# Second SSD layer, beginning: six stores for twenty, rows before totals, first masked copy behind the C tile

## The chip, the cores and the metric

The kernel runs on one core of a Trainium2 chip. Its time is device microseconds (us) of one execution. The core's engines work side by side, each through its own list of instructions in order: TensorE (PE in the profile, with PEld for its weight loads), VectorE (DVE), ScalarE (ACT), GpSimd (POOL), and SyncE (SP), which here issues DMA transfers and little else. An instruction starts when those ahead of it on its engine have started and the semaphores it waits for are there.

## The reference, cut to what matters

Two layers over 1024 latent and 256 context tokens, width 1024. The first is windowed attention, the second a bidirectional Mamba-2 (SSD) mixer. The change is in the second alone. Per direction d (0 forward, 1 backward) and chunk of 128 tokens it computes:

```python
dt = softplus(dt_raw + dt_bias)                    # 2 directions x 32 heads
a_cs = cumsum(dt * a, axis=chunk)                  # the decays
a_last = a_cs[:, :, -1]                            # the totals, one per chunk
states = einsum(bm, exp(a_last - a_cs), x * dt)
h_next = exp(a_last) * h + states                  # over chunks; context chunks come first
lmat = exp(where(lower, a_cs[q] - a_cs[s], -inf))  # 128 x 128 per head
y = (cm . bm) * lmat . (x * dt)  +  (cm . h) * exp(a_cs)
```

`x`, `bm` and `cm` come from one projection, a depthwise convolution over five tokens and a SiLU. There are 32 heads in 8 groups of 4, head width 64, state width 128, and 8 latent and 2 context chunks.

## The kernel before, in words

All matrix products of the projections are done three times, with a high and a low part of each operand (`wh`, `wl`, `uH`, `uL`). The second layer works group by group. `front(g)` is a generator that issues the projection of group g, one TensorE product at a time: the B tile (`bT`), two x tiles (`cacc`), the C tile (`cT`), then the gate z (L1129). For the B and x tiles a context part (`psD`, `cctx`) goes with the latent part (`pj2`, shown as `pj`). Behind each tile come the steps of `taps` (one ScalarE activation, four VectorE taps, L1007 and L1011), `silu` (a ScalarE tanh, L1018, and a VectorE product, L1019) and, for B and x, `natural` (TensorE transposes, L1058, and ScalarE copies out, L1061, to `xn` and `bn`). These steps wait in a queue `post`, from which `run(cost)` takes as the projection goes on.

The recurrence is in `states` (eleven jobs a group). A job is a weighting on GpSimd (`xw`, L1173), a TensorE product (`psD`, L1198), and for the first of a direction a ScalarE copy (`hx`, L1202), for the others a GpSimd decay by `eal` (L1178) and a VectorE addition (L1210). Then `slot(n)` computes the output of one chunk. It needs the matrix of decays `M`: per chunk two 256 KB loads from DRAM, `M` for the forward rows and `bw` for the backward rows, each row of `acs` broadcast over 128 partitions. GpSimd shifts `bw` (`offset`, L1226), VectorE copies `bw` into `M` under a mask (`merge`, L1230, COPY_PREDICATED), ScalarE takes four exponentials (`decays`, L1236). M and bw have two buffers each, and so have the weights `wr`, `wh`, `wl`.

Only once, while group 0 is projected, `dt_chain` makes the decays of all groups. Two VectorE scans (L986 for direction 0 on partitions 0 to 63, L987 for direction 1 on 64 to 127) write `w3` (named `sz` in the trace). Its 640 columns are five blocks of 128 tokens: two latent, one context, two latent, so that a partition row holds half a head's tokens. `decay` stores it to the DRAM tensor `acs` (64 rows of 1024); `total` takes each chunk's last value, its exponential `et` (named `tot`) is stored to the DRAM tensor `eald`, and one load (L953) brings this to all partitions as `eal`. `rows` asks for the rows of the first two chunks. Everything is float32. After the projection of group 0 the function `ssd` flushes `post`, finishes `states` and merges the first chunk's rows ahead of the loop over groups.

The order within an engine is not that of the code alone: a planner lays out each engine's list by dependences, code order and its own timeline, and `issue_after(x)` asks it to place an instruction behind x on x's engine, with no wait added.

Of the kernel before, what the change touches and what calls it, by code (L numbers as in the profile page):

```python
# [12 lines left out]
AF = mybir.ActivationFunctionType  # L13
ALU = mybir.AluOpType
# [3 lines left out]
P = 128  # L18
# [15 lines left out]
R = 4  # L34
HP = 64
# [24 lines left out]
OUT = 4 * 30 * 3 * N512  # L60
POST = 0.5
LATE = 3.0
DTPACE = 1.0
SEGS = (1.5, 2.0, 2.0, 2.2, 2.2)
_STOP = None
# [46 lines left out]
class Kernel:  # L112
# [13 lines left out]
    def t(self, pool, shape, dt, tag, bufs=None):  # L126
        self.n += 1
        kw = {"bufs": bufs or BUFS.get(tag, 1)}
        return pool.tile(shape, dt, tag=tag, name=f"{tag}_{self.n}", **kw)
# [795 lines left out]
    def dt_chain(self, keep, rows):  # L925

        nc, t, ps, p = self.nc, self.t, self.psA, self.ps_
        n = 640
        nb = n // P
        dt = self.dts  # L930
        w1, w2, w3, ea = [t(p, [P, KT // 2, 256], F32, y).rearrange("p a b -> p (a b)")[:, :n] for y in ("xn4", "sz", "sz", "xn4")]
        tot = t(self.pc, [P, 8], F32, "tot", 2)[:, :nb]
        et = t(self.pc, [P, 8], F32, "tot", 2)[:, :nb]
        blocks = lambda x: x.rearrange("p (c n) -> p c n", n=P)
        v, act = nc.vector, nc.scalar.activation

        def decay():
            for o in (0, 384):
                for y in range(4):
                    d, s = y // 2, (o // 384) * 512 + 256 * (y % 2)  # L940
                    nc.sync.dma_start(self.acs_d[32 * d : 32 * d + 32, s : s + 256], w3[32 * y : 32 * y + 32, o : o + 256])

        def total():
            v.tensor_copy(tot[:64], blocks(w3)[:64, :, P - 1])
            v.tensor_copy(tot[64:], blocks(w3)[64:, :, 0])
            act(et, tot, AF.Exp)
            for y in range(4):
                d, h = y // 2, y % 2
                row = self.eal_d[0][32 * d : 32 * d + 32]
                for o, c in ((0, 2 * h), (3, 4 + 2 * h)):  # L950
                    nc.sync.dma_start(row[:, c : c + 2], et[32 * y : 32 * y + 32, o : o + 2])
                nc.sync.dma_start(row[:, 8 + h : 9 + h], et[32 * y : 32 * y + 32, 2:3])
            nc.sync.dma_start(self.eal, self.eal_d.broadcast_to([P, 64, NCH + NCC]))  # L953

        def pairs(tile, d, c, step):
            return tile[:, c : c + step + 1 : step, 32 * d : 32 * d + 32]

        def turn(b):
            sl = slice(b * P, (b + 1) * P)
            c, step = {0: (0, 2), 1: (1, 2), 2: (8, 1), 3: (4, 2), 4: (5, 2)}[b]  # L960
            pt = t(ps, [P, 512], F32, "psX").rearrange("p (k d h r) -> p k d h r", k=4, d=2, h=2)
            srcs = (w1, ea, dt, w2) if c < NCH else (w1,)
            for k, src in enumerate(srcs):
                nc.tensor.transpose(pt[:, k].rearrange("p d h r -> p (d h r)"), src[:, sl], self.ident)
            for d in range(2):
                nc.scalar.copy(pairs(self.dtdec, d, c, step), pt[:, 0, d])
                if c < NCH:
                    nc.scalar.copy(pairs(self.eacs, d, c, step), pt[:, 1, d])
            if c < NCH:
                nc.scalar.copy(pairs(self.dtb, 0, c, step), pt[:, 2, 1])  # L970
                nc.scalar.copy(pairs(self.vf, 0, c, step), pt[:, 3, 0])
                nc.vector.tensor_sub(pairs(self.vd, 0, c, step), pt[:, 3, 1], pairs(self.vf, 0, c, step))

        steps = [
            lambda: v.scalar_tensor_tensor(w1, in0=dt, scalar=-1.0, in1=dt, op0=ALU.mult, op1=ALU.min),
            lambda: act(w1, w1, AF.Exp),
            lambda: v.tensor_scalar_add(w2, w1, 1.0),
            lambda: v.tensor_scalar_add(w3, w2, -1.0),
            lambda: (act(ea, w2, AF.Ln), v.tensor_sub(w1, w1, w3)),
            lambda: v.reciprocal(w3, w2),  # L980
            lambda: v.tensor_mul(w1, w1, w3),
            lambda: v.tensor_add(w1, w1, ea),
            lambda: v.scalar_tensor_tensor(dt, in0=dt, scalar=0.0, in1=w1, op0=ALU.max, op1=ALU.add),
            lambda: v.tensor_scalar_max(w2, dt, 1.0e-38),
            lambda: (act(w2, w2, AF.Ln), v.tensor_scalar(out=w1, in0=dt, scalar1=self.aneg, scalar2=None, op0=ALU.mult)),
            lambda: v.tensor_tensor_scan(out=w3[:64], data0=keep[:64], data1=w1[:64], initial=0.0, op0=ALU.mult, op1=ALU.add),  # L986
            lambda: v.tensor_tensor_scan(out=w3[64:, ::-1], data0=keep[64:, ::-1], data1=w1[64:, ::-1], initial=0.0, op0=ALU.mult, op1=ALU.add),  # L987
            decay,
            total,
            lambda: v.tensor_sub(blocks(w1), tot.unsqueeze(2).broadcast_to([P, nb, P]), blocks(w3)),  # L990
            lambda: act(w1, w1, AF.Exp),
            lambda: v.tensor_sub(w2, w2, w3),
            lambda: v.tensor_mul(w1, w1, dt),
            lambda: act(ea, w3, AF.Exp),
            rows,
        ]
        return steps + [lambda b=b: turn(b) for b in (2, 0, 4, 3, 1)]

    def dt_tail(self, raw, post, keep, rows):

        self.dt_raw(self.dts[:, 384:], raw, 256)
        post.extend([(DTPACE * x, [f]) for x, f in enumerate(self.dt_chain(keep, rows))])

# [11 lines left out]
    def silu(self, raw, acc):  # L1015

        nc = self.nc
        return [lambda: nc.scalar.activation(raw, acc, AF.Tanh),  # L1018
                lambda: nc.vector.scalar_tensor_tensor(acc, in0=raw, scalar=1.0, in1=acc, op0=ALU.add, op1=ALU.mult)]  # L1019

    def front(self, g, st, post, first=None, dt=None):

# [20 lines left out]
        def need(w):  # L1043
            while "l" not in w:
                post.pop()
# [7 lines left out]
        def natural(raw, acc, dst, o, n):  # L1053
# [6 lines left out]
            def ev(d, lo, hi):  # L1060
                nc.scalar.copy(d[:, :, o : o + P], raw[:, lo * P : hi * P].rearrange("p (c n) -> p c n", n=P))  # L1061

            for d, lo, hi in dst:
                steps.append(lambda lo=lo, hi=hi: tr(lo, hi))
                steps.append(lambda d=d, lo=lo, hi=hi: ev(d, lo, hi))
            return [(LATE, steps)]

# [8 lines left out]
        for n, (x, kind) in enumerate(tiles):  # L1076
# [37 lines left out]

            post.append((LATE, [done]) if nat else done)
        need(w)
# [28 lines left out]
    def ssd(self, c0):  # L1145
        nc, t, a = self.nc, self.t, self.a
# [9 lines left out]
        for x in range(2):  # L1156
            y = t(ps2, [P, 260], F32, f"y{x}")
# [4 lines left out]
        def hd(d, g):  # L1162
            return slice(32 * d + 4 * g, 32 * d + 4 * g + 4)
# [11 lines left out]
            return xw  # L1175

        def decay(hn, h, g, c, d):
            nc.gpsimd.tensor_tensor(hn, h, self.eal[:, hd(d, g), c].unsqueeze(2).broadcast_to([P, R, HP]), op=ALU.mult)  # L1178

        def flat(x):  # L1180
            return x.rearrange("p r h -> p (r h)")
# [1 line left out]
        def states(g, st):  # L1183
# [5 lines left out]
            for n, (d, c) in enumerate(jobs):  # L1189
                if n == 0:  # L1190
                    xw[0] = xweight(st, g, c, d)
                    yield
                if n + 1 < len(jobs):
                    xw[n + 1] = xweight(st, g, jobs[n + 1][1], jobs[n + 1][0])
                else:
                    st["xw"] = xweight(st, g, 0, 0)
                s = t(ps, [P, 512], F32, "psD")[:, :256]
                nc.tensor.matmul(s, B(st, c), flat(xw.pop(n)), start=True, stop=True)  # L1198
                sv = s.rearrange("p (r h) -> p r h", r=R)
                if n in (0, 2):  # L1200
                    h = t(ps2, [P, R, HP], F32, "hx")
                    nc.scalar.copy(h, sv)  # L1202
                else:
                    if n == 1:
                        hn = t(ps2, [P, R, HP], F32, "hf0")
                    else:
                        o = NCH - 1 if n == 3 else c - 1
                        hn = t(ps2, [P, R, HP], F32, f"hb{o if g % 2 == 0 else NCH - 1 - o}")
                    decay(hn, h, g, c, d)
                    nc.vector.tensor_add(hn, hn, sv)  # L1210
                    if n == 1:
                        st["hf"] = hn
                    else:
                        st["hb"][o] = h = hn
                yield
# [8 lines left out]
        def offset(n, bw):  # L1224
            g, c = divmod(n, NCH)
            nc.gpsimd.tensor_tensor(bw, bw, self.vd[:, c, 4 * g : 4 * g + 4].unsqueeze(2).broadcast_to([P, R, P]), op=ALU.add)  # L1226

        def merge(M, bw):

            nc.vector.copy_predicated(M, self.before.unsqueeze(1).broadcast_to([P, R, P]), bw)  # L1230
# [89 lines left out]
        fw, bw = {}, {}  # L1320
# [18 lines left out]
        for _ in chain:  # L1339
            pass  # L1340
        offset(0, bw[0])
        merge(fw[0], bw.pop(0))
        for half in range(2):
            decays(0, fw[0], half)
        self.tail = None
# [348 lines left out]
```

## Time and profile before

| | |
|---|---|
| median of three runs | 1809.46 us (1806.79 to 1813.08) |
| profiled execution | 1807.02 us, span 1805.3 us |
| TensorE busy | 1739.6 us (96%) |
| VectorE, ScalarE, GpSimd busy | 1181.8, 867.1, 799.0 us |
| mean granted TensorE clock | 0.993 |
| eight decay stores issued (SP) | from 794.12 us on |
| twelve stores of totals issued | 798.35 to 803.8 us |
| first row load issued | 803.93 us |
| load of `eal` issued, landed | 806.68 us, 8.0 us later |
| first masked copy | 815.05 us |

Times in the trace are us from the span's start. A timeline row has start, duration, engine, line, operation, out<-in, shapes and count; in brackets stands the idle time of the engine before it and what ended it. Buffer numbers are left out of names, so `pj` is any buffer of `pj2`. The chain of waits follows the last instruction back to what released it. Matmul ends are modelled, and rows of the same line and tile that follow each other are merged. A DMA's landing is counted from its issue.

### The profile page before, as it was taken

What the parts mean: (1) busy time and instruction counts of PE and PEld (TensorE: products, weight loads), DVE (VectorE), ACT (ScalarE), POOL (GpSimd) and SP (SyncE); (2) the same over time, 40 slices, a digit from 0 to 9 for tenths busy, and PEclk for the clock granted to TensorE, in tenths of its full rate; (3) what the DMA queues carried; (4) which work ended last, traced back from release to release, by engine and by line L of the source; (5) the groups of instructions that cost most, each with busy time, mean ns of one, the idle gap of its engine ahead of it and who ended that gap; (6) DMA issues with size and microseconds to landing.
All of it is one profiled execution on the core that took longest, in us unless ns stands there. A gap on an engine that the chain in (4) does not pass through costs nothing.

```text
span 1805.3 us, 28983 instructions
## 1 busy us (share of the span) xinstructions
PE 1739.6 (96%) x10319; PEld 1494.7 (83%) x10319; DVE 1181.8 (65%) x2115; ACT 867.1 (48%) x1906; POOL 799.0 (44%) x1068
## 2 busy tenths in 40 slices
PE   6899999999999999999999999999999999999997
PEld 2697788888888887778888898988889898888887
DVE  4634436778877885684776858577684867766734
ACT  3612237777777774452443525344353534544522
POOL 2331127555575545103454544645454464554411
PEclk9999999999999999999999999999999999999999
DMA  9558856444455436222222323222332322656533
GB/s 334 226 144 268 283 177 149 106 100 111 111 153 130 120 102 221 73 53 73 71 77 82 92 62 98 79 71 79 81 93 62 100 73 76 174 169 170 175 101 121
DMA packets 212495, 227.61 MB, mean 126 GB/s; under 512 B 16384, under 2 KB 149632, under 8 KB 212352
## 3 DMA queue, kind: packets, MB, share of 16 engines
q1 hardware_dynamic: 178288, 207.12, 38.0%
q0 software_dynamic: 34064, 18.65, 5.8%
q8 instruction: 81, 1.33, 0.3%
q14 instruction: 62, 0.51, 0.1%
HBM read 190.88 MB, written 35.13 MB: 125 GB/s over the span
## 4 chain that ended last, share of the span: by engine, by line
PE 81%; DVE 9%; ACT 4%; DMA 3%; issue 2%; SPq 1%; POOL 1%; DVEq 0%; ACTq 0%; POOLq 0%
PE pj L1095 17%; PE pj L1129 10%; PE pj L1527 7%; PE pj L246 6%; PE pj L247 6%; PE pj L248 6%; PE psD L1085 4%; PE psX L1281 3%; PE pt L684 3%; PE psD L1198 2%; PE pv L691 2%; PE pv L690 1%; PE S L659 1%; PE S L658 1%; PE psX L1249 1%
## 5 line engine op out<-in xcount | busy, mean ns | idle before, releaser
L246 PE MATMUL pj<-uH,wh 128*128 128x512 f32 (+1 forms) x712 | 257.4, 363 | 9.0 <-ACT uH L470 6.3
L247 PE MATMUL pj<-uL,wh 128*128 128x512 f32 (+1 forms) x712 | 243.3, 342 | 0.5 <-POOL uL L707 0.4
L248 PE MATMUL pj<-uH,wl 128*128 128x512 f32 (+1 forms) x712 | 242.4, 341 | 1.4 <-POOL wl L231 1.4
L1095 PE MATMUL pj<-uH,wl 128*128 128x512 f32 x512 | 172.7, 405 | 0.0
L1095 PE MATMUL pj<-uH,wh 128*128 128x512 f32 x512 | 171.4, 405 | 1.2 <-ACT bn L1061 0.7
L1095 PE MATMUL pj<-uL,wh 128*128 128x512 f32 x512 | 169.2, 402 | 0.0
L246 PEld LDWEIGHTS pj<-uH,wh 128*128 128x128 f32 x712 | 135.6, 191 | 36.2 <-ACT uH L470 7.7
L1129 PE MATMUL pj<-wh,uH 128*128 128x256 f32 x512 | 150.3, 294 | 9.1 <-ACT xn L1061 9.1
L1173 POOL TENSOR_TENSOR xw<-xn,dtdec 128x256 f32<-128x256 f32 x144 | 92.9, 650 | 141.6 <-PE psD L1198 107.1
L1129 PE MATMUL pj<-wh,uL 128*128 128x256 f32 x512 | 152.7, 298 | 0.0
L248 PEld LDWEIGHTS pj<-uH,wl 128*128 128x128 f32 x712 | 135.0, 190 | 18.6 <-POOL wl L231 2.3
L247 PEld LDWEIGHTS pj<-uL,wh 128*128 128x128 f32 x712 | 135.8, 191 | 16.0 <-issue 3.0
L1129 PE MATMUL pj<-wl,uH 128*128 128x256 f32 x512 | 146.7, 287 | 0.0
L689 DVE TENSOR_TENSOR pl<-pt,ph 128x512 fp32r<-128x512 f32 x168 | 114.1, 688 | 47.2 <-ACT ph L688 46.2
L231 POOL TENSOR_TENSOR wl<-wr,wh 128x512 fp32r<-128x512 f32 x76 | 100.2, 1322 | 86.1 <-ACT wh L229 85.2
L663 DVE CUSTOM_DVE_ANT_0 sm<-S,mask,nsink 128x640 f32<-128x640 f32 (+2 forms) x160 | 119.2, 773 | 19.8 <-PE S L659 12.6
L665 ACT ACTIVATE sm<-sm,nm 128x640 f32<-128x640 f32 (+2 forms) x160 | 118.6, 742 | 16.6 <-DVE nm L663 15.9
L688 ACT CAST ph<-pt 128x512 fp32r<-128x512 f32 x168 | 97.5, 586 | 56.0 <-PE pt L684 52.7
L229 ACT CAST wh<-wr 128x512 fp32r<-128x512 f32 (+1 forms) x116 | 74.7, 648 | 87.7 <-PE pj L247 63.5
L1095 PEld LDWEIGHTS pj<-uH,wl 128*128 128x128 f32 x512 | 95.3, 188 | 19.2
L1095 PEld LDWEIGHTS pj<-uL,wh 128*128 128x128 f32 x512 | 95.4, 188 | 18.7
L1129 PEld LDWEIGHTS pj<-wh,uH 128*128 128x128 f32 x512 | 98.7, 193 | 13.5 <-ACT xn L1061 12.1
(339 smaller groups left out, 4810.8 us busy)
## 6 DMA issues: line engine op xcount, KB each, us to landing
wr<-w_x SPq DMA_DIRECT2D x32, 512.0 KB, 4.6
M<-acs SPq DMA_DIRECT2D x64, 256.0 KB, 4.9
bw<-acs SPq DMA_DIRECT2D x64, 256.0 KB, 5.5
wr<-w_sk SPq DMA_DIRECT2D x24, 512.0 KB, 3.8
wr<-wg SPq DMA_DIRECT2D x40, 256.0 KB, 4.5
qs<-q POOLq DMA_DIRECT2D x40, 256.0 KB, 3.9
wada<-w_ada SPq DMA_DIRECT2D x16, 512.0 KB, 7.2
wr<-wq SPq DMA_DIRECT2D x32, 256.0 KB, 3.0
```

Of the source, the lines that this page charges most:

```text
L231: (eng or nc.vector).tensor_tensor(l, raw, h, op=ALU.subtract)
L246: self.nc.tensor.matmul(ps, lh, rh, start=first and i == 0, stop=False)
L247: self.nc.tensor.matmul(ps, lh, rl, start=False, stop=False)
L248: self.last_mm = self.nc.tensor.matmul(ps, ll, rh, start=False, stop=last and i == n - 1)
L663: nc.vector.tensor_tensor_reduce(out=sm[:, :W], in0=Sv, in1=self.mask[:, m0 : m0 + W], scale=-SCALE, scalar=self.nsink[:, 4 * j + r : 4 * ...
L665: nc.scalar.activation(sm[:, :W], sm[:, :W], AF.Exp, bias=nm[:, r : r + 1], scale=-1.0, accum_out=sums[:, r : r + 1])
L688: nc.scalar.copy(ph, ptf)
L689: nc.vector.tensor_sub(pl, ptf, ph)
L1095: nc.tensor.matmul(raw[:, 512 * i : 512 * i + 512], l[:, k, :], r[i][:, k, :], start=k + y == 0, stop=k == KT - 1 and y == 2)
L1129: nc.tensor.matmul(pj[:, c], l, r[:, k, :], start=c % 2 + q + k + y == 0, stop=c % 2 == 1 and q == 1 and k == 3 and y == 2)
L1173: nc.gpsimd.tensor_tensor(xw, X(st, c).rearrange("p (r h) -> p r h", r=R), self.dtdec[:, c, hd(d, g)].unsqueeze(2).broadcast_to([P, R, HP] ...
L1527: nc.tensor.matmul(banks[x], l[:, z, sl], r, start=k == 2 * qs[0] and y == 0, stop=k == 2 * qs[-1] + 1 and y == 2)
```

## The change

`decay` and `total` store two blocks, or five totals, of all 64 rows of a direction in one transfer: four stores of 2x32x256 for eight of 32x256, and two of 2x32x5 for twelve of 32x2 and 32x1. The totals lie in `eald` in the order of the blocks, and `EPOS` gives the column of each chunk. `rows` moves from the end of the chain to a place between `decay` and `total`. `silu` keeps its last product in `self.silu_last`, and the first chunk's `merge` is put behind it with `issue_after`; the last such product of the flush is the C tile's.

```diff
+EPOS = (0, 1, 5, 6, 3, 4, 8, 9, 2, 7)
...
         def decay():
-            for o in (0, 384):
-                for y in range(4):
-                    d, s = y // 2, (o // 384) * 512 + 256 * (y % 2)
-                    nc.sync.dma_start(self.acs_d[32 * d : 32 * d + 32, s : s + 256], w3[32 * y : 32 * y + 32, o : o + 256])
+            for d in range(2):
+                for o in range(2):
+                    dst = self.acs_d[32 * d : 32 * d + 32, 512 * o : 512 * o + 512].rearrange("r (h n) -> h r n", h=2)
+                    nc.sync.dma_start(dst, w3[64 * d : 64 * d + 64, 384 * o : 384 * o + 256])
...
             act(et, tot, AF.Exp)
-            for y in range(4):
-                d, h = y // 2, y % 2
-                row = self.eal_d[0][32 * d : 32 * d + 32]
-                for o, c in ((0, 2 * h), (3, 4 + 2 * h)):
-                    nc.sync.dma_start(row[:, c : c + 2], et[32 * y : 32 * y + 32, o : o + 2])
-                nc.sync.dma_start(row[:, 8 + h : 9 + h], et[32 * y : 32 * y + 32, 2:3])
+            for d in range(2):
+                nc.sync.dma_start(self.eal_d[0, 32 * d : 32 * d + 32].rearrange("r (h k) -> h r k", h=2), et[64 * d : 64 * d + 64])
             nc.sync.dma_start(self.eal, self.eal_d.broadcast_to([P, 64, NCH + NCC]))
...
             decay,
+            rows,
             total,
...
             lambda: act(ea, w3, AF.Exp),
-            rows,
         ]
...
-        return [lambda: nc.scalar.activation(raw, acc, AF.Tanh),
-                lambda: nc.vector.scalar_tensor_tensor(acc, in0=raw, scalar=1.0, in1=acc, op0=ALU.add, op1=ALU.mult)]
+
+        def prod():
+            self.silu_last = nc.vector.scalar_tensor_tensor(acc, in0=raw, scalar=1.0, in1=acc, op0=ALU.add, op1=ALU.mult)
+
+        return [lambda: nc.scalar.activation(raw, acc, AF.Tanh), prod]
...
-            nc.gpsimd.tensor_tensor(hn, h, self.eal[:, hd(d, g), c].unsqueeze(2).broadcast_to([P, R, HP]), op=ALU.mult)
+            nc.gpsimd.tensor_tensor(hn, h, self.eal[:, hd(d, g), EPOS[c]].unsqueeze(2).broadcast_to([P, R, HP]), op=ALU.mult)
...
         offset(0, bw[0])
-        merge(fw[0], bw.pop(0))
+        with self.tc.issue_after(self.silu_last.ins):
+            merge(fw[0], bw.pop(0))
```

In the built programs the lists of TensorE and GpSimd are the same in both. SP's list from the last stores of totals on, before (names are the program's tiles with their numbers; `wr<-w_x` are weight loads):

```order
L951 DMA eald_8741<-tot_8874 32x2 x2
L952 DMA eald_8741<-tot_8874 32x1
L1221 DMA M_9099<-acs_8737 128x4x128
L1221 DMA bw_9101<-acs_8737 128x4x128
L953 DMA eal_8736<-eald_8741 128x640
L1221 DMA M_9103<-acs_8737 128x4x128
L1221 DMA bw_9105<-acs_8737 128x4x128
L1030 DMA wr_9536<-w_x 128x1024
L1221 DMA bw_9599<-acs_8737 128x4x128
L1030 DMA wr_9620<-w_x 128x1024
```

and SP's list from the stores of the decays on, now:

```order
L942 DMA acs_8737<-sz_8871 2x32x256 x4
L1221 DMA M_9003<-acs_8737 128x4x128
L1221 DMA bw_9005<-acs_8737 128x4x128
L1221 DMA M_9007<-acs_8737 128x4x128
L1221 DMA bw_9009<-acs_8737 128x4x128
L949 DMA eald_8741<-tot_8874 2x32x5 x2
L950 DMA eal_8736<-eald_8741 128x640
L1030 DMA wr_9522<-w_x 128x1024
L1030 DMA wr_9606<-w_x 128x1024
L1221 DMA bw_9585<-acs_8737 128x4x128
```

All four row loads now stand ahead of the stores of the totals, and the third chunk's `bw` stands behind one weight load more.

VectorE's list from the first masked copy on, before (`cacc_9091` is the second x tile, `cT_9227` the C tile):

```order
L1230 COPY_PREDICATED M_9099<-before_8738,bw_9101 128x512
L972 TENSOR_TENSOR vd_8732<-psX_9179,vf_8731 128x2x32
L972 TENSOR_TENSOR vd_8732<-psX_9198,vf_8731 128x2x32
L1019 SCALAR_TENSOR_TENSOR cacc_9091<-pj_2194_9090,cacc_9091 128x1024
L1038 TENSOR_TENSOR wl_9331<-wr_9318,wh_9329 128x1024
L1011 SCALAR_TENSOR_TENSOR cT_9227<-pj_2208_9226,cw_8721,cT_9227 128x1022
```

and VectorE's list from the x tile's product to the same copy, now:

```order
L1017 SCALAR_TENSOR_TENSOR cacc_9084<-pj_2198_9083,cacc_9084 128x1024
L1038 TENSOR_TENSOR wl_9317<-wr_9304,wh_9315 128x1024
L1008 SCALAR_TENSOR_TENSOR cT_9213<-pj_2208_9212,cw_8721,cT_9213 128x1022
L1008 SCALAR_TENSOR_TENSOR cT_9213<-pj_2208_9212,cw_8721,cT_9213 128x1023
L1210 TENSOR_TENSOR hf_2218_9283<-hf_2218_9283,psD_9281 128x256
L1008 SCALAR_TENSOR_TENSOR cT_9213<-pj_2208_9212,cw_8721,cT_9213 128x1023
L1008 SCALAR_TENSOR_TENSOR cT_9213<-pj_2208_9212,cw_8721,cT_9213 128x1022
L1017 SCALAR_TENSOR_TENSOR cT_9213<-pj_2208_9212,cT_9213 128x1024
L1230 COPY_PREDICATED M_9003<-before_8738,bw_9005 128x512
L1210 TENSOR_TENSOR hb_2228_9326<-hb_2228_9326,psD_9324 128x256
```

The copy has moved from ahead of the x tile's product to behind the C tile's. ScalarE's list, before, from the tanh of the x tile on:

```order
L1018 ACTIVATE pj_2194_9090<-cacc_9091 128x1024
L1236 ACTIVATE M_9099<-M_9099,vf_8731 128x128 x4
L1061 COPY xn_2160_8759<-psD_9056 128x2x128
L1034 CAST wh_9329<-wr_9318 128x1024
L1007 ACTIVATE cT_9227<-pj_2208_9226,cb_8724,cw_8721 128x1024
```

and ScalarE's list from the context copy on, now:

```order
L1061 COPY xn_2160_8759<-psD_9049 128x2x128
L1034 CAST wh_9315<-wr_9304 128x1024
L1004 ACTIVATE cT_9213<-pj_2208_9212,cb_8724,cw_8721 128x1024
L1061 COPY xn_2158_8757<-pj_2198_9083 128x4x128
L1202 COPY hx_9270<-psD_9268 128x256
L1061 COPY xn_2159_8758<-pj_2198_9083 128x4x128
L1019 ACTIVATE pj_2208_9212<-cT_9213 128x1024
L1202 COPY hx_9297<-psD_9295 128x256
L1236 ACTIVATE M_9003<-M_9003,vf_8731 128x128 x4
L1137 ACTIVATE sz_9463<-pj_2223_9306 128x1024
```

The four exponentials have moved from ahead of the context copy to behind the second state copy. Nothing else moves on either engine.

## The prediction

> **What bounds the kernel.** First the page: TensorE works 96% of the span, so only what lets it stand, or run at a lower clock, counts.
>
> ```profile
> PE 1739.6 (96%) x10319; PEld 1494.7 (83%) x10319; DVE 1181.8 (65%) x2115; ACT 867.1 (48%) x1906; POOL 799.0 (44%) x1068
> ```
>
> All that the change touches lies between 794 and 832 us, so next I read the chain that ended last there, in order of time (start, us, what).
>
> ```profile
> 807.07 9.10 DMA M<-acs
> 816.17 0.97 ACT M L1236 x3
> ...
> 817.30 1.04 ACT wh L1034
> 818.35 1.10 ACT cT L1007
> 819.45 0.48 ACT xn L1061
> ...
> 819.98 1.12 PE pj L1058 x4
> ...
> 821.95 5.08 PE pj L1129 x30
> ...
> 831.73 2.87 PE pj L1129 x24
> ```
>
> The chain leaves TensorE for a transfer, runs through ScalarE and comes back at 819.98. The timelines of TensorE, VectorE, ScalarE and GpSimd (start, us, operation, and in brackets the idle time ahead of it) tell why.
>
> ```profile
> 814.26 0.62 PE L1095 MATMUL pj<-uH,wl 128*128 128x512 f32 x2
> 817.19 0.66 PE L1058 MATMUL pj<-ident,cacc 128*128 128x128 f32 x4 [2.31 <-DVE cacc L1019]
> 818.14 1.22 PE L1198 MATMUL psD<-xw,bn 128*128 128x256 f32 x2 [0.29 <-POOL xw L1173]
> 820.88 1.06 PE L1198 MATMUL psD<-xw,bn 128*128 128x256 f32 x2
> 821.77 0.58 PE L1129 MATMUL pj<-wh,uH 128*128 128x256 f32 x1
> ```
>
> ```profile
> 808.52 1.27 DVE L1011 SCALAR_TENSOR_TENSOR cacc<-pj,cw,cacc 128x1022 f32<-128x1022 f32 x1
> 815.05 0.73 DVE L1230 COPY_PREDICATED M<-before,bw 128x512 f32<-128x512 int32 x1 [5.26 <-POOL bw L1226]
> ...
> 815.92 1.22 DVE L1019 SCALAR_TENSOR_TENSOR cacc<-pj,cacc 128x1024 f32<-128x1024 f32 x1
> ...
> 819.67 2.59 DVE L1011 SCALAR_TENSOR_TENSOR cT<-pj,cw,cT 128x1022 f32<-128x1022 f32 x2
> 822.17 0.41 DVE L1210 TENSOR_TENSOR hf<-hf,psD 128x256 f32<-128x256 f32 x1
> ...
> 831.83 0.42 DVE L1210 TENSOR_TENSOR hb<-hb,psD 128x256 f32<-128x256 f32 x1 [4.36 <-PE psD L1198]
> ```
>
> ```profile
> 810.73 1.10 ACT L1018 ACTIVATE pj<-cacc 128x1024 f32<-128x1024 f32 x1
> 815.87 1.28 ACT L1236 ACTIVATE M<-M,vf 128x128 f32<-128x128 f32 x4 [4.04 <-DVE M L1230]
> 817.05 0.35 ACT L1061 COPY xn<-psD 128x256 f32<-128x256 f32 x1
> ...
> 836.26 1.02 ACT L1137 ACTIVATE sz<-pj 128x1024 f32<-128x1024 f32 x1 [8.39 <-PE pj L1129]
> ```
>
> ```profile
> 813.97 1.04 POOL L1226 TENSOR_TENSOR bw<-bw,vd 128x512 f32<-128x512 f32 x1 [72.63 <-DMA bw<-acs]
> 817.48 1.19 POOL L1173 TENSOR_TENSOR xw<-xn,dtdec 128x256 f32<-128x256 f32 x2 [2.47 <-ACT xn L1061]
> ...
> 820.27 0.62 POOL L1178 TENSOR_TENSOR hf<-hx,eal 128x256 f32<-128x256 f32 x1
> ```
>
> The first masked copy (L1230) waits on VectorE for rows that are still in flight; the product of the x tile (L1019, cacc) stands behind it in order, and TensorE's transposes wait for that product 2.31 us. ScalarE waits 4.04 us for the copy too, with the context copy (817.05) and all that follows queued behind its four exponentials. There is a second price, in the windows of TensorE (length, then busy time of PE, PEld, DVE, ACT, POOL, granted clock, DMA share, GB/s):
>
> ```profile
> 781.00:785.00 4.00, 1.72 (x11) 0.86 (x9) 4.00 (x6) 3.18 (x4) 0.00 (x0) 1.00 0.00 0
> 814.76:818.17 3.41, 0.80 (x6) 0.45 (x5) 2.09 (x4) 2.30 (x6) 0.94 (x3) 1.00 0.58 104
> 818.17:821.58 3.41, 2.80 (x8) 1.72 (x8) 3.17 (x3) 2.48 (x5) 1.88 (x3) 0.50 0.73 208
> 821.58:824.99 3.41, 3.41 (x16) 3.23 (x16) 3.38 (x4) 0.13 (x1) 1.24 (x2) 0.50 0.48 177
> ```
>
> After the stretch with 0.80 us of work the granted clock is 0.50 for 6.8 us.
>
> **The change, part by part.** *Masked copy moved.* VectorE's product now needs only the tanh, which ends at 810.73 + 1.10 = 811.83, and VectorE, free from 809.8 but for two small subtractions. It runs from 811.9 to 813.1, before TensorE is free at 814.26 + 0.62 = 814.88. So the first transposes start at 814.9 and the 2.31 us are gone. Late next is ScalarE. Its weight cast (817.30) takes the buffer that the product of the C tile reads until about 814.5, and cannot start sooner; from it to the second transposes are 819.98 - 817.30 = 2.68 us, so those start at 817.2, **2.8 us** earlier. From them to the first L1129 are 821.77 - 819.98 = 1.79 us at half clock; at full clock four transposes take 0.66 (row 817.19), the copy that follows some 0.57, with handing over 1.3. L1129 starts at 818.5, 3.3 earlier: **0.5 us** more. The fifteen L1129 matmuls up to 825.0 (the last window has sixteen, one of them a state product's) took 3.22 us; at the full rate, 2.87 / 24 = 0.12, they take 1.80: **1.4 us** more.
>
> The clock term rests on there being no drop: from 814.9 TensorE has transposes (0.4 to 0.66) and a state product (0.43 at full clock), then about 1.3 us of waiting up to 817.2. It is then busy some 2.0 of 3.41 us (59%). The stretch from 781 to 785 was busy 1.72 of 4.00 (43%) and kept its clock at 1.00.
>
> *Where the copy goes.* It costs VectorE 0.73 us after the C tile's product, and the exponentials cost ScalarE 1.28. Behind it in VectorE's order stands the addition that idled 4.36 us (831.83), behind the exponentials the tanh that idled 8.39 us (836.26). Both covers are longer than the cost, also 4.7 us earlier since TensorE's products, which they wait for, move along. Were the cover gone, the price would be 0.73 and 1.28. The next row load (bw of the third chunk) waits for the copy and goes behind one weight load on SP's queue; it is used only in the second chunk, tens of us later: nothing.
>
> *Stores and rows on SP's queue.* Prices come from the DMA view, issues by tile (size, median us to landing), packets in two short windows (packets, MB, share of 16 engines), and SP's own rows:
>
> ```profile
> M<-acs SPq DMA_DIRECT2D x64, 256.0 KB, 4.9
> ...
> h<-h SPq DMA_DIRECT2D x16, 256.0 KB, 2.6
> ...
> wr<-w_x SPq DMA_DIRECT2D x32, 512.0 KB, 4.6
> ```
>
> ```profile
> q1 hardware_dynamic: 246, 0.12, 96.0%
> ```
>
> ```profile
> q1 hardware_dynamic: 96, 0.07, 13.5%
> ...
> acs<-sz SPq DMA_DIRECT2D x4, 32.0 KB, 1.5
> ```
>
> ```profile
> 794.12 4.14 SPq L941 DMA_DIRECT2D acs<-sz  x8
> ...
> 803.93 0.39 SPq L1221 DMA_DIRECT2D M<-acs  x1
> ```
>
> Twenty stores are twenty issues of about 0.42 us on SP (803.93 - 794.12 = 9.8 us with the gaps); six cost about 3. No engine waits for SP's issuing itself, so the saving counts only in when rows and totals land. Four decay stores go out from 794.1, the last two after the second scan (795.6), and land by 796.2 + 1.5 = 797.7. The rows are asked for then, 6 us sooner, and are no longer late for anything. The totals pay: their stores are queued behind four row loads of 512 packets. In the window from 807.5 to 809 such packets passed at 246 in 1.5 us, 3.1 us a load; so the fourth lands 4.9 + 3 x 3.1 = 14.2 us after the first is issued, the totals' stores 1.4 us later at most, and the load of eal takes 2.6 to 4.6 us (the rows of 256 and 512 KB; it has 320). From 797.7 that is 815.9 to 817.9. eal is first read by GpSimd's decay (820.27 before, about 817.5 now); its result, 0.62 on GpSimd and 0.42 on VectorE later, must be there when TensorE comes to the third state product, thirty L1129 after 818.5, at 822.1. So eal may land as late as 820.9 at no cost: I take nothing, and keep 0 to 2.8 us for the range (rival A). Reading eal by another column changes no size.
>
> Sum: 2.8 + 0.5 + 1.4 = **4.7 us** less. After 825 TensorE works on without a gap to 832 and everything behind hangs on it, so the shift is kept. The profiled execution took 1807.02 us (span 1805.30 and 1.7 around it), which gives 1802.3; it lies 2.4 us under the median of three, 1809.46, and against the median it is **1804.8 us**. A difference under 0.3% (5.4 us) can hardly be told here from no change: the three runs alone span 6.3 us.
>
> **Rivals.** *A, totals late, gain partly lost.* Each new store has the target form 2x32x256 against 64 source rows. If its 64 packets go out on two DMA engines and not sixteen, they queue: 96 packets took 13.5% of 16 x 2 us, 45 ns each, or 67 ns if the 32 tiny ones took none. Four stores then need 4 x 32 x 0.045 to 0.067 = 5.8 to 8.6 us from the first packet at about 794.95, the rows start at 800.7 to 803.5, and eal lands at 818.9 to 823.7. Beyond 820.9 each us is one us of TensorE: 0 to 2.8, middle 1.4, time 1806.2 us. For it speaks the shape; against it that no store here shows such a queue and the margin of 3 us. The Trainium skill (DMA: Bandwidth & Descriptors, section "Why a DMA increments its semaphore by 16 and not by 1") states that a transfer is split over the largest number of engines up to 16 that divides the slowest dimension of both sides, here 2 and 64, hence two engines. No run so far shows this, and by that rule rival A's landing holds instead of 817.
>
> *B, slower.* The same queue past the point where it takes all: eal landing after 820.9 + 4.7 = 825.6. One engine for all four stores would do it: 4 x 64 x 0.045 to 0.067 = 11.5 to 17.2 us, eal at 824.7 to 832.3, a stall of 3.8 to 11.4 us in which the clock falls again (another 1.4): net 0.5 to 8.1 us slower, middle 4, time 1813.5 us. Against it: the stores' target has two halves.
>
> *C, the clock falls all the same.* With 59% busy the granted clock may still drop at some 818.2 and stay for 6.8 us; 6.5 us of L1129 at half rate lose 3.25, leaving 4.7 - 3.2 = 1.5: 1808.0 us. For it: 43% is one case only. The Trainium skill (TensorE: Matmul & The Clock Gate, "Part 1: The HAM clock gate") has a free-running window of about 3.4 us; twice 3.41 us in the trace agrees. By that rule the phase differs between runs, and a run of the old kernel without the drop would leave a gain of 2.8.
>
> **How the numbers follow.** Forecast 0.57, A 0.25, C 0.10, B 0.08. The forecast's 1804.8 is 0.8 us short of the bound at 1804.0, and the profiled execution suggests that the median of before is a high one, so I give it a little over even odds of passing the bound (0.33), A a third (0.08), C little (0.01): faster 0.42. B gives slower, and noise a little more: 0.09. The rest, 0.49, is within 0.3%. Range: runs scatter by 3 us around a median, so 1800.3 below; above it takes in A, C and B's near end, 1810.0.
>
> **What would show it.** In the changed kernel's timeline: the x tile's product on VectorE near 812 with no wait for bw; the first transposes at once behind the C tile's matmuls; the second near 817; L1129 at 0.12 us from the start and a granted clock of 1.00 throughout; the copy idle-free behind the C tile's product. The landing of eal decides A and B: GpSimd's first decay waits for a DMA if it is late, and TensorE's third state product waits behind it. I would be wrong if decay stores take longer than 3 us more to land, or if something after 850, hung on a transfer and not on TensorE, eats the shift.

## The result, and the profile after

The changed kernel took 1806.33 us in the median of 19 runs (1801.31 to 1811.95), the kernel before 1811.43 us in the median of 19 runs (1805.89 to 1814.45). The ratio of the runs is 0.9977, with a 95% interval of 0.9968 to 0.9986: 4.2 us less (2.5 to 5.8). This ratio, and not the quotient of the two medians, which lie 5.1 us apart, is used below. The forecast was 4.7 us less than a median of 1809.46. The interval holds 4.7 us, but also the 2.8 that the wait alone would give; how the gain is made up is read from traces, one of each kernel.

The profiled execution after took 1801.31 us, span 1799.6, which is 5.7 us under the span before. Of these, 1.8 us were there before the change begins: the second decay scan starts at 792.30 and not at 794.12, after a first layer that ran a little faster. The changed stretch gave 4.7, and the very end took 0.8 back (below). So the changed stretch is read against the second scan: a time that was forecast on the trace of before is met if the new trace shows it 1.82 us earlier.

TensorE's share in the page, then the chain that ended last (start, us, what), in the kernel after:

```profile
PE 1736.7 (97%) x10319; PEld 1493.0 (83%) x10319; DVE 1180.8 (66%) x2115; ACT 867.6 (48%) x1906; POOL 797.9 (44%) x1068
```

```profile
812.62 0.49 ACT wh L1034
...
813.57 1.20 ACT cT L1004
814.77 0.48 ACT xn L1061
...
815.30 0.67 PE pj L1058 x4
...
815.99 0.60 ACT xn L1061
...
816.63 3.86 PE pj L1129 x30
820.49 0.43 PE psD L1198 x2
...
842.92 0.22 PE psX L1247 x2
```

No transfer stands in it any more. It leaves TensorE at 812.6 for ScalarE's cast, the C tile's activation and one copy, and is back for good at 816.63. The first and the second transposes are two groups of four products (L1058) on the second x tile. The timelines of TensorE, VectorE, ScalarE and GpSimd after, at the places that the prediction named:

```profile
812.88 0.60 PE L1058 MATMUL pj<-ident,cacc 128*128 128x128 f32 x4
...
815.30 0.66 PE L1058 MATMUL pj<-ident,cacc 128*128 128x128 f32 x4 [1.38 <-ACT xn L1061]
...
816.63 0.39 PE L1129 MATMUL pj<-wh,uH 128*128 128x256 f32 x1 [0.24 <-ACT xn L1061]
```

```profile
810.02 1.23 DVE L1017 SCALAR_TENSOR_TENSOR cacc<-pj,cacc 128x1024 f32<-128x1024 f32 x1 [0.71 <-ACT pj L1019]
...
821.70 1.22 DVE L1017 SCALAR_TENSOR_TENSOR cT<-pj,cT 128x1024 f32<-128x1024 f32 x1 [1.43 <-ACT pj L1019]
822.84 0.74 DVE L1230 COPY_PREDICATED M<-before,bw 128x512 f32<-128x512 int32 x1
825.30 0.42 DVE L1210 TENSOR_TENSOR hb<-hb,psD 128x256 f32<-128x256 f32 x1 [1.72 <-PE psD L1198]
```

```profile
823.61 1.28 ACT L1236 ACTIVATE M<-M,vf 128x128 f32<-128x128 f32 x4 [1.64 <-DVE M L1230]
829.73 1.02 ACT L1137 ACTIVATE sz<-pj 128x1024 f32<-128x1024 f32 x1 [4.83 <-PE pj L1129]
```

```profile
804.93 1.04 POOL L1226 TENSOR_TENSOR bw<-bw,vd 128x512 f32<-128x512 f32 x1 [66.95 <-DVE vd L969]
...
815.60 0.62 POOL L1178 TENSOR_TENSOR hf<-hx,eal 128x256 f32<-128x256 f32 x1 [0.20 <-ACT hx L1202]
```

The x tile's product (cacc, 810.02) waits for its tanh alone, the first transposes (812.88) follow the C tile's products without a wait, and the idle time that is left on TensorE is 1.38 us ahead of the second transposes, for ScalarE's copy. The copy under the mask (822.84) stands behind the C tile's product, and both engines still idle behind it, 1.72 and 4.83 us. GpSimd's shift of bw (804.93) waited for VectorE's `vd` and no longer for a transfer, and its first decay (815.60) for ScalarE's `hx`, not for `eal`.

TensorE's windows after (columns as before):

```profile
812.00:815.41 3.41, 2.03 (x12) 1.41 (x11) 1.72 (x2) 2.79 (x4) 2.49 (x3) 1.00 0.13 54
815.41:818.82 3.41, 3.17 (x24) 2.77 (x25) 3.37 (x4) 0.69 (x2) 1.86 (x3) 1.00 0.54 154
```

The emptiest stretch is busy 2.03 of 3.41 us, and the granted clock stays at 1.00.

SP's issues after:

```profile
792.30 2.54 SPq L942 DMA_DIRECT2D acs<-sz  x4
795.90 0.38 SPq L1221 DMA_DIRECT2D M<-acs  x1
799.36 0.38 SPq L1221 DMA_DIRECT2D bw<-acs  x1
...
800.33 0.51 SPq L1221 DMA_DIRECT2D bw<-acs  x1
800.88 2.16 SPq L949 DMA_DIRECT2D eald<-tot  x2
807.07 0.34 SPq L950 DMA_DIRECT2D eal<-eald  x1
```

The DMA view after, packets from 793.4 to 796.9, and below it of before, from 794.5 to 796.5:

```profile
DMA packets 120, 0.12 MB, mean 34 GB/s; under 512 B 3, under 2 KB 120, under 8 KB 120
...
q1 hardware_dynamic: 120, 0.12, 12.7%
```

```profile
DMA packets 105, 0.07 MB, mean 37 GB/s; under 512 B 32, under 2 KB 105, under 8 KB 105
```

The window of after holds stores of decays only: 12.7% of 16 engines is 2.0 engines' worth, and among 120 packets 3 are small ones; before, 32 of 105 were. In the trace's single packets each new store is two streams of 46 ns a packet of 1 KB, one packet behind another, with two small completion writes where a store before had sixteen. The four stores' last packet passes at 800.2. The first row load is issued at 795.90, while the stores still run: the first store's completion writes passed at 795.39 and 795.48, and the load waits only for the store of its own quarter of `acs`. The one for `bw` waits until 799.36.

What the end took back is in the chain, TensorE's last two products, before and then after:

```profile
1796.82 0.71 PE psX L380 x2
```

```profile
1790.23 1.24 PE psX L381 x2
```

The same two products took 0.53 us more. Before, the granted clock fell to 0.50 only at 1797.79, behind them; after, it fell at 1789.12, ahead of them. Nothing of the change lies there; the stretch is nearly idle in both.

### The profile page after: what moved, and what is told of

Its sections match the earlier page's. It is cut to its first block, busy times and chain, and to the rows that moved or that the text cites. A ratio compares the mean times of both kernels' runs of the same rounds, so it can differ in the third digit from the quotient of the medians.

```text
span 1799.6 us, 28962 instructions
## 1 busy us (share of the span) xinstructions
PE 1736.7 (97%) x10319; PEld 1493.0 (83%) x10319; DVE 1180.8 (66%) x2115; ACT 867.6 (48%) x1906; POOL 797.9 (44%) x1068
## 3 DMA queue, kind: packets, MB, share of 16 engines
q8 instruction: 81, 1.33, 0.3%
## 4 chain that ended last, share of the span: by engine, by line
PE 81%; DVE 9%; ACT 4%; DMA 2%; issue 2%; POOL 0%; SPq 0%; DVEq 0%; ACTq 0%; POOLq 0%
PE pj L1095 18%; PE pj L1129 10%; PE pj L1528 7%; PE pj L247 6%; PE pj L248 6%; PE pj L249 6%; PE psD L1085 4%; PE pt L685 3%; PE psX L1281 3%; PE pv L692 2%; PE psD L1198 2%; PE pv L691 2%; PE S L660 1%; PE S L659 1%; PE psX L1249 1%
## 5 line engine op out<-in xcount | busy, mean ns | idle before, releaser
L1129 PE MATMUL pj<-wh,uH 128*128 128x256 f32 x512 | 149.6, 292 | 9.4 <-ACT xn L1061 9.4
L1129 PE MATMUL pj<-wh,uL 128*128 128x256 f32 x512 | 152.1, 297 | 0.0
L1129 PE MATMUL pj<-wl,uH 128*128 128x256 f32 x512 | 146.1, 285 | 0.0
L1129 PEld LDWEIGHTS pj<-wh,uH 128*128 128x128 f32 x512 | 98.0, 191 | 13.7 <-ACT xn L1061 12.2
```

The source lines that it names most:

```text
L1129: nc.tensor.matmul(pj[:, c], l, r[:, k, :], start=c % 2 + q + k + y == 0, stop=c % 2 == 1 and q == 1 and k == 3 and y == 2)
```

## The experiments

What a kernel did to the changed stretch is measured from the start of the second decay scan (VectorE) to the start of the first chunk's first product (TensorE, L1247): behind it TensorE's timeline shows no wait for the next 70 us in either trace. In TensorE's timeline this is 55.17 us before and 50.45 after, 4.72 less. (The expectations give 55.33 and 50.62, which are the chain's rows for the same product; the chain starts it 0.16 later.) Before, after and three of the others were timed in many runs, the rest in one, where only the stretch is read; in all, the stretch is that of one traced execution. In the table all columns but the last are us after the start of the second scan.

| kernel | first L1129 | third state product | first chunk's product | masked copy | first decay by `eal` | ratio to before |
|---|---|---|---|---|---|---|
| before | 27.65 | 32.75 | 55.17 | 20.93 | 26.15 | |
| after | 24.33 | 28.03 | 50.45 | 30.54 | 23.29 | 0.9977 [0.9968, 0.9986] |
| place of the copy alone | 24.36 | 28.05 | 50.48 | 30.77 | 23.85 | 0.9986 [0.9973, 0.9999] |
| after without that place | 24.35 | 28.05 | 50.48 | 13.80 | 23.31 | 0.9974 [0.9961, 0.9987] |
| six stores alone | 26.27 | 30.28 | 52.71 | 17.12 | 24.92 | one run |
| rows early alone | 24.35 | 28.05 | 50.48 | 14.24 | 24.68 | one run |
| after, totals three copies later | 24.33 | 28.03 | 50.45 | 31.12 | 24.96 | one run |
| after, totals six copies later | 24.35 | 32.39 | 56.41 | 37.42 | 31.26 | one run |
| before, the wait filled with products | 27.69 | 32.11 | 53.81 | 21.41 | 26.66 | one run |
| after, second copy ahead of the activation | 23.76 | 26.98 | 49.89 | 30.73 | 23.30 | 0.9964 [0.9949, 0.9980] |

### The copy's place alone

On the kernel before, only the masked copy is put behind the C tile's product; stores and rows stay.

```diff
-        merge(fw[0], bw.pop(0))
+        with self.tc.issue_after(self.silu_last.ins):
+            merge(fw[0], bw.pop(0))
```

> The kernel before with one edit alone: the first masked copy behind the C tile's product; twenty stores and late rows stay. Measure: from the start of the second scan on VectorE to the first product of the first chunk on TensorE (L1247), 55.33 us before and 50.62 in the changed kernel. Theory: the copy's place in VectorE's list is the cause and is enough; bw lands as late as before, GpSimd's shift of it ends near 815 and the weighting that follows is late by under 1 us, which is hidden: 50.6 to 51.2 us, and about 0.2% off the time. Rival: the late rows still bind through GpSimd, whose shift of bw stands ahead of the weighting: 52.5 us or more, at most half of the gain.

Measured: 50.48, all of the stretch's gain, and 0.9986 of the time before. GpSimd's shift still waits for its rows, and delays the weighting behind it:

```profile
813.75 1.04 POOL L1229 TENSOR_TENSOR bw<-bw,vd 128x512 f32<-128x512 f32 x1 [72.92 <-DMA bw<-acs]
```

```profile
815.42 0.70 PE L1201 MATMUL psD<-xw,bn 128*128 128x256 f32 x2 [0.61 <-POOL xw L1176]
816.62 0.66 PE L1061 MATMUL pj<-ident,cacc 128*128 128x128 f32 x4 [0.51 <-ACT xn L1064]
```

TensorE waits 0.61 us for the weighting, but the second transposes (816.62) would have had to wait for ScalarE anyway. Late rows cost nothing once the copy does not stand ahead of the x tile's product.

### Stores and rows, without the copy's place

The changed kernel with the masked copy where the planner puts it.

```diff
-        with self.tc.issue_after(self.silu_last.ins):
-            merge(fw[0], bw.pop(0))
+        merge(fw[0], bw.pop(0))
```

> The changed kernel without the new place of the copy: six stores and early rows alone. Theory: what was paid was the wait for bw, not the copy; with bw there by about 806 the copy and its exponentials fit into idle time of VectorE and ScalarE before the x tile's tanh and product: 50.6 to 51.6 us in the measure, and about 0.2% off the time, so that either half of the change does the whole. Rival: the copy (0.73 us) and the four exponentials (1.28) stay in the chain to TensorE, or both halves are needed: 52.5 us or more.

Measured: 50.48 again, and 0.9974 of the time before. The copy now runs on VectorE well ahead of the x tile's product (cacc, L1017):

```profile
807.60 0.74 DVE L1230 COPY_PREDICATED M<-before,bw 128x512 f32<-128x512 int32 x1 [0.84 <-POOL bw L1226]
...
812.12 1.23 DVE L1017 SCALAR_TENSOR_TENSOR cacc<-pj,cacc 128x1024 f32<-128x1024 f32 x1 [0.80 <-ACT pj L1019]
```

The planner put the copy two taps of the x tile further ahead than before, and its exponentials ahead of the x tile's tanh; the copy still waits 0.84 us there, at no cost to TensorE. So the 0.73 us of the copy were never the price; its wait was. (That it was not the place in the list is shown by six stores alone, below: there the copy stands in the same place, waits 4.18 us, and half of the gain is gone.) Either half of the change makes that wait harmless, and with both nothing is gained over one.

### Rows early alone, six stores alone

Of that half, the two parts one by one: the kernel before with only `rows` moved between `decay` and `total`, and the kernel before with only the six stores.

```diff
             decay,
+            rows,
             total,
...
             lambda: act(ea, w3, AF.Exp),
-            rows,
         ]
```

> Early rows alone: twenty stores of the old form, rows between the decay stores and the totals, copy in no new place. Theory: rows are asked for at about 798, bw lands by 806, no wait: 50.6 to 51.6 us in the measure; each old decay store's data is down within 0.2 us of its first packet, against more than 1 us for a new one. The twelve stores of totals behind the rows bring eal some 4 us later than in the changed kernel, still hidden. Rival: totals late enough to hold TensorE: 52.5 us or more, with GpSimd's first decay waiting for a DMA.

> Six stores alone: rows asked for behind the totals' stores, copy in no new place. Theory: SP is free for the first rows some 4 us sooner, bw lands by about 808 and the copy waits for nothing: 50.6 to 51.6 us in the measure. Rival: the six stores land so late, each on few DMA engines, that the copy still waits for bw and TensorE with it: 53 us or more.

Rows early alone gave 50.48, the whole; the copy, in the same place as above, waited 1.28 us. Its totals, in twelve stores behind four row loads, came so late that GpSimd's first decay waited for them, at no cost to TensorE:

```profile
821.96 0.62 POOL L1178 TENSOR_TENSOR hf<-hx,eal 128x256 f32<-128x256 f32 x1 [1.44 <-DMA eal<-eald]
```

Six stores alone gave 52.71, half of the gain, which neither theory had expected. Here the rows are asked for behind the totals, and the wait is shorter but still there. GpSimd, VectorE and the windows of TensorE in that kernel:

```profile
809.70 1.04 POOL L1226 TENSOR_TENSOR bw<-bw,vd 128x512 f32<-128x512 f32 x1 [70.37 <-DMA bw<-acs]
```

```profile
810.78 0.74 DVE L1230 COPY_PREDICATED M<-before,bw 128x512 f32<-128x512 int32 x1 [4.18 <-POOL bw L1226]
...
815.29 1.23 DVE L1017 SCALAR_TENSOR_TENSOR cacc<-pj,cacc 128x1024 f32<-128x1024 f32 x1 [0.80 <-ACT pj L1019]
```

```profile
813.85:817.26 3.41, 1.23 (x8) 0.79 (x7) 2.60 (x5) 3.41 (x8) 1.18 (x2) 1.00 0.54 187
817.26:820.68 3.42, 3.21 (x11) 2.00 (x10) 3.38 (x5) 1.68 (x4) 1.69 (x3) 0.50 0.47 137
820.68:824.09 3.41, 3.41 (x30) 3.41 (x29) 2.54 (x3) 0.74 (x1) 0.74 (x2) 1.00 0.05 19
```

The copy stands ahead of two taps of the x tile, so its wait of 4.18 us pushed those taps, the tanh and the product (815.29); TensorE waited 2.18 us for that product. The clock fell too, at 817.26, but came back at 820.68, after 3.42 us and not 6.83. Of the 2.46 us gained, 1.38 are there at the first L1129 (26.27 for 27.65 in the table). The other 1.08 are gained between it and the first chunk's product, where the drop ended sooner.

### How late the totals may be

The changed kernel with three, or six, extra copies of the totals' tensor between their stores and the load of `eal`; they compute nothing.

```diff
-            nc.sync.dma_start(self.eal, self.eal_d.broadcast_to([P, 64, NCH + NCC]))
+            last = self.eal_d
+            for x in range(3):      # or 6
+                hop = t(self.dr, [1, 64, NCH + NCC], F32, f"hop{x}")
+                nc.sync.dma_start(hop, last)
+                last = hop
+            nc.sync.dma_start(self.eal, last.broadcast_to([P, 64, NCH + NCC]))
```

> The changed kernel, with the totals passed through three more DRAM tensors, one copy after another, before eal is loaded: a delay of about 2 us each with hardly any traffic. In the changed kernel eal's packets end 19.3 us after the second scan's start, and TensorE's third state product comes 28.2 us after it, so eal may land up to 26.9 us after. Theory (the break-even of the prediction): at about 25.5 nothing is lost, 50.6 us in the measure. Rival (totals have no slack): every us of delay costs one: 56 us.

> The same with six more copies: eal lands about 31.5 us after the second scan's start, 4.5 past the point. Theory: the measure grows by landing less 26.9 us, to about 55, and by up to 1.4 more if the granted clock falls in the stall; GpSimd's first decay waits for a DMA and TensorE's third state product behind it. Rival (the totals are read later than I think, or another wait hides them): 50.6 us.

With three copies the first decay waits 1.87 us for the load and nothing is lost: 50.45. With six it waits 8.14 us. GpSimd, TensorE and TensorE's windows with six (the state product is L1203 here, the gate's products L1134):

```profile
821.31 0.62 POOL L1183 TENSOR_TENSOR hf<-hx,eal 128x256 f32<-128x256 f32 x1 [8.14 <-DMA eal<-hop]
```

```profile
822.44 0.70 PE L1203 MATMUL psD<-xw,bn 128*128 128x256 f32 x2 [4.18 <-DVE hf L1215]
```

```profile
819.65:823.06 3.41, 0.62 (x3) 0.57 (x4) 1.09 (x2) 0.00 (x0) 1.75 (x3) 1.00 0.53 180
823.06:826.48 3.42, 3.42 (x18) 3.42 (x17) 1.95 (x3) 1.21 (x2) 0.64 (x2) 0.50 0.01 2
```

The third state product comes at 32.39 in place of 28.03, 4.36 late, for a decay at 31.26. A decay at 31.26 - 4.36 = 26.9 would have been just in time; in the changed kernel it stands at 23.29, a margin of 3.6 us. The whole stretch lost 5.96 us, 1.6 more than the stall, and the windows show the second price: the clock at 0.50 for 3.42 us behind it.

### The clock's term by itself

On the kernel before, eight products of 128x512 that nothing reads are put on TensorE where it waits for the x tile's product. They take nothing of the copy's wait away; they only keep TensorE busy in it.

```diff
+            if g == 0 and kind == "cT":
+                fill = t(ps, [P, 512], F32, "psX")
+                for k in range(KT):
+                    nc.tensor.matmul(fill, wh[:, k, :], uH[0][:, k, :], start=k == 0, stop=k == KT - 1)
```

> The kernel before, with eight products of 128x512 that nobody reads (1.84 us) put on TensorE behind the C tile's own, in the gap in which it waited 2.31 us for the x tile. The waits stay. Theory: what the gap cost beyond its length is the granted clock; with the gap filled the clock stays at 1.00, the second transposes start as before, and L1129 runs at 0.12 us from the start: 0.5 + 1.4 = 1.9 us less, 53.4 us in the measure. Rival (the clock falls anyway, or costs nothing): 55.3 us.

Measured: 53.81, that is 1.36 us less. TensorE and its emptiest window:

```profile
818.21 1.99 PE L1111 MATMUL psX<-uH,wh 128*128 128x512 f32 x8
...
821.22 0.66 PE L1058 MATMUL pj<-ident,cacc 128*128 128x128 f32 x4 [1.02 <-DVE cacc L1019]
...
824.00 0.66 PE L1058 MATMUL pj<-ident,cacc 128*128 128x128 f32 x4 [1.13 <-ACT xn L1061]
```

```profile
821.32:824.73 3.41, 1.98 (x12) 1.30 (x12) 2.13 (x2) 2.94 (x6) 2.23 (x4) 1.00 0.49 163
```

The granted clock stays at 1.00, and the gate's products take 0.12 us from the first one. The wait itself was 0.5 us longer in this execution: the rows of `bw` came later after the scan, GpSimd's shift began at 20.34 and not 19.85, and with it the masked copy (21.41 for 20.93) and both groups of transposes (the second at 26.36 for 25.86). From there on both terms that the clock was expected to give are seen: from the second transposes to the first gate product 1.33 us in place of 1.79 (the 0.5), and from that product to the first chunk's 26.12 in place of 27.52 (the 1.4). They add to 1.86 us, against the 1.9 expected. The planner also changed ScalarE's order here, the weight cast behind the C tile's activation, but from the first transposes to the second it is 2.78 us, where it was 2.79. (The third state product stands six L1129 further on in this kernel's list, and four fewer in the list of the table's last row, so this column can't be compared for these two.)

### What is late next

In the changed kernel ScalarE does the cast, then the C tile's activation, then the copy that the second transposes wait for. Here the activation goes behind that copy.

```diff
-                nc.scalar.copy(d[:, :, o : o + P], raw[:, lo * P : hi * P].rearrange("p (c n) -> p c n", n=P))
+                self.ev = nc.scalar.copy(d[:, :, o : o + P], raw[:, lo * P : hi * P].rearrange("p (c n) -> p c n", n=P))
+                if lo == 0 and hi == 4:
+                    self.ev_first = self.ev
...
-            post.extend(self.taps(x, raw, acc, 0, LAT, LAT) + self.silu(raw, acc))
+            steps = self.taps(x, raw, acc, 0, LAT, LAT)
+            if g == 0 and kind == "cT":
+                start = steps[0]
+
+                def behind(start=start):
+                    with self.tc.issue_after(self.ev_first.ins):
+                        start()
+
+                steps[0] = behind
+            post.extend(steps + self.silu(raw, acc))
```

> The changed kernel with one more move on ScalarE: the C tile's first activation (1.2 us) behind the copy that the second transposes wait for. Theory: the second transposes and L1129 start about 0.8 us sooner, the C tile's taps 0.5 us later and hidden: 49.8 us in the measure, a time not to be told from the changed kernel's. Rival: the state addition and the third state product are late behind the C tile's taps: 50.6 us or more.

Measured: 49.89, 0.56 us less than the changed kernel's stretch. TensorE there:

```profile
814.67 0.66 PE L1058 MATMUL pj<-ident,cacc 128*128 128x128 f32 x4 [0.28 <-ACT xn L1061]
816.13 0.67 PE L1209 MATMUL psD<-xw,bn 128*128 128x256 f32 x2 [0.80 <-ACT hx L1213]
```

The second transposes wait 0.28 and not 1.38 us; part of that comes back as 0.80 ahead of the state product, which now waits for the `hx` copy behind the activation. Ahead of the first gate product no wait is left, where it was 0.24. The kernel took 1804.48 us in the median of 8 runs, against 1811.03 before in 13 on the same chip. It is the fastest kernel of this study in the changed stretch, but its ratio, 0.9964 with an interval of 0.9949 to 0.9980, can't be told from the changed kernel's 0.9977.

## Why the prediction was right, and where its working was off

**The sum.** 4.7 us were forecast, and the changed stretch gave 4.72: 2.86 up to the second transposes, 0.46 from them to the first L1129, 1.40 behind it, against 2.8, 0.5 and 1.4. Taken 1.82 us back, the second transposes were due at 815.4 and came at 815.30; the first L1129 was due at 816.7 and came at 816.63; the third state product was due at 820.3 and came at 820.49. The whole time moved by 4.2 us (2.5 to 5.8). The forecast lay just inside the 0.3%, and so does the measured 0.23%.

**The three terms.** The wait for the copy (2.8 us) is shown by the two kernels that remove it in different ways and gain the same. The clock's two terms (0.5 and 1.4) are shown by the filled wait, which left the wait in place: 0.46 and 1.40. Each is read from one execution. The drop begins and ends where the trace's clock changes, and these times lie differently in each execution: it lasted 6.83 us before and 3.42 with six stores alone. So the 1.4 is the price in the traced execution of the kernel before; no second trace of that kernel shows what it is in others, and whether it has runs without the drop, for which rival C gives a gain of 2.8, stays open.

**No drop of the clock (rival C).** The windows bear the forecast's 59% out: 2.03 of 3.41 us busy, clock at 1.00. But the reading that such a share is safe was partly luck. In this same trace of after, long ahead of the change, the clock fell behind a window busy 2.18 of 3.41 us, and the trace of before kept it at the like place with 2.31:

```profile
734.40:737.82 3.42, 2.18 (x15) 1.92 (x15) 1.23 (x1) 3.36 (x7) 0.85 (x1) 1.00 0.51 146
737.82:741.23 3.41, 3.41 (x10) 2.62 (x9) 1.83 (x2) 0.09 (x1) 0.17 (x1) 0.50 0.66 191
```

The Trainium skill (TensorE: Matmul & The Clock Gate, "Part 1: The HAM clock gate") has the clock fall after an idle window of about 3.4 us. The traces show a fall behind windows that were not idle but busy 0.80 of 3.41 us (before), 1.23 (six stores alone) and 0.62 (six copies); they agree with the page on the window's length, not on its being idle.

**The copy's new place.** It cost nothing, with 1.72 and 4.83 us of idle time left behind it on VectorE and ScalarE.

**The totals: right in the sum, wrong in the working.** The step that said that four decay stores land by 797.7 took the 1.5 us of the old 32 KB stores for the new ones of 64 KB. The stores went out on two engines, as rival A had it; their last packet passed at 800.2, or 802.0 in the times of before. That is 4.3 us later, and the prediction had named more than 3 us as a sign that it would be wrong. That it held all the same is luck as far as its working goes. Two engines each worked for the whole transfer, and the Trainium skill (DMA: Bandwidth & Descriptors, "Why a DMA increments its semaphore by 16 and not by 1") had said so: the trace agrees, with two completion writes a store. By rival A's sum `eal` should then have landed at 818.9 or later, and that did not happen either, for two reasons. First, the rows did not wait for all four stores; each load waited for its own quarter, and the first went out at 795.90. Second, the rows passed faster than the 3.1 us a load that the sum took: 1767 of their 2048 packets had passed by 805.4. The totals' 20-byte packets passed from 805.4 to 805.9, and `eal` was asked for at 807.07. Its packets passed from 808.2 to 811.6, 2.5 us ahead of the forecast's window (814.1 to 816.1 in the times of after). Both errors were of the landing and fell inside the margin. The margin itself was right: a break-even at 820.9, or 26.8 after the scan, against the 26.9 that six copies showed.

**The old median.** That the three runs' median was a high one was wrong: nineteen runs put it at 1811.43.

**What the prediction did not see.** It credited the change as a whole. The change's two halves each remove the same wait, and the six stores are needed by neither: rows early alone gave all. What the six stores do buy is a margin, since without them the totals already waited 1.44 us.

## What to carry to other kernels

When a wait stands in front of the bound engine, look for all the ways to take it away and try each by itself: here the waiting instruction could be moved, or what it waits for could be asked for earlier, and one was enough. Cost the wait with the clock: in the traced execution a TensorE gap of 2.3 us cost 1.9 us more behind it, and work that nobody reads, put in the gap, won that back. And here merging stores into a form with a small leading dimension (2x32x256) saved nothing for the DMA engines, only for the queue that issues them.

## What the runs showed of the hardware

- A store whose target form is 2x32x256 ran as two streams of 1 KB packets at 46 ns: four of 64 KB were under way from 793.5 to 800.2, where a 32x256 store before passed its 32 packets within some 0.25 us. Fewer issues, longer transfers.
- The changes of the granted clock in a trace lie whole steps of 3.41 us apart: it was low for 6.83 us before and for 3.42 us with six stores alone and with six copies. Counted in those steps, in all ten traces, it fell behind every step in which TensorE was busy 1.66 us or less, and behind none busy more than 2.30. Between 1.68 and 2.30 us it fell behind some steps and not behind others, so the busy time alone does not decide there.
- Once low, the clock came back behind every step busy 2.88 us or more, and behind none busy 2.80 or less. Before, TensorE was busy 2.80 us in the first low step (818.17 to 821.58), and the clock stayed low for a second one; with six stores alone the first low step was busy 3.21 us.
- Packets of the row loads (512 B) took very different times: 0.96 x 16 x 1.5 us / 246 = 94 ns before in the window that the prediction quotes, and 0.837 x 16 x 1 us / 476 = 28 ns after, from 804 to 805, by this row of the DMA view:

```profile
q1 hardware_dynamic: 476, 0.24, 83.7%
```

In the kernel with rows early alone both rates occur one after the other, 107 to 161 packets a us from 803 to 809 and 503 in the next us. What makes the difference stays open; an estimate of 3.1 us a load from the slow window was the wrong term here.
